# Where attention stops and retention starts: three steps further apart, deferred work kept for its own phase, and retention's first loads in another order

## The chip, the cores and the metric

The kernel runs on one core of one Trainium2 chip, as one launch. The metric is the device time in microseconds (us), as the median of several executions. A core has a matrix engine (PE, with its weight loads shown as PEld), three engines for element work (DVE, ACT, POOL), and a sequencer (SP) that here does nothing but issue DMAs; ACT issues a few DMAs of its own. Each engine takes its instructions in order.

## The reference

One layer that mixes two branches over a sequence of 2048 rows of 1024 columns, all in float32:

```python
h = rms_norm(x, norm_gain[l])
proj = jnp.einsum('bsd,df->bsf', h, w_in[l])
q_a, k_a, v_a, g_a, q_r, k_r, v_r, g_r, m_a, m_r = split_columns(proj)
o_a = chunk_band_attention(q_a, k_a, v_a, rel_bias[l])      # own chunk of 64 rows and 8 to the left, 8 heads
branch_a = (o_a * silu(g_a)) @ w_out_attn[l]
o_r = retention_chunkwise(rotary(q_r), rotary(k_r), v_r, gn_gain[l])   # 8 heads, state carried along the rows
branch_r = (o_r * silu(g_r)) @ w_out_ret[l]
mixed = sigmoid(m_a) * branch_a + sigmoid(m_r) * branch_r
x = x + mixed @ w_out[l]
out = rms_norm(x, final_gain)
```

(Reshapes are left out.) In `retention_chunkwise` the scores of a chunk are multiplied by a decay mask, and a state of 64 by 128 per head goes from chunk to chunk.

## The kernel before, in words

**Two kinds of work share PE.** The large projections are "dense" work: `p0` and `p1` make queries, keys and values of the first and of the second half of the rows, `g0` and `g1` the gates, and `ba`, `br` and `out` the three output products. Each float32 operand is kept as a high and a low part, so one *dense step* is three matmuls of 128x512. A `Strassen` job has chunks of seven products, a product has four steps, and `g0` and `g1` have 14 chunks, thus 392 steps each. Between the dense steps stands the work of attention (`attention`, once for each half of the rows) and of retention (`retention`, likewise). Attention's and retention's Python code emits its own instructions and calls `fill(n)`, which emits n dense steps (fractions are carried in `credit`, of which at most 1.0 is kept). So the order on PE is written out by the program: attention of the first half beside `g0`, then retention of the first half beside the rest of `g0`, and the same for the second half with `g1` and the start of `ba0`.

**What a step leaves for later.** Work that follows a matmul on another engine is put off by whole dense steps: `later(n, fn)` puts `fn` into the list `deferred`, and `step()` runs what is due before it emits the next dense step. A gate's chunk works this way (`ep_gate`: ACT's tanh, DVE's product, and a DMA of the result eight steps later), and so does everything in attention and retention. `flush()` empties the whole list at once. It is called where a phase ends, since the buffers of the phase (`E` tiles, `tr` banks) are given back there: at the end of `p0`, of attention, of retention, of `p1`.

**Refilling the resident operand.** The right-hand operand `R` (seven blocks of 128x4x512, high `r..0` and low `r..1`) stays in the core. While the last chunk of `g0` runs, `reload(n)` refills each block for `p1` as soon as its last product is done: a DMA into the low part (tile `r`), seven or more steps later ACT's copy to the high part, and two steps after that the subtraction on DVE or (every third) on POOL. `fill_yr` does the same at the end of `g1`.

**Attention's end.** `attention` works on units of 256 rows of one head. The last product of a unit (`po`) is emitted `PV_LAG` = 3 steps after its operands, and then ACT, DVE and POOL make the output `oa`, which a DMA writes 6 steps later. `attention` ends with `fill(PV_LAG + 2)`.

**Retention.** `retention` goes over pairs of heads p and stretches st of 256 rows; each of the two heads is an item, 32 in all. For an item PE makes the scores `sr` from `kr` and `qr`; DVE multiplies by the mask `dm` (`sm`), ACT copies the high part (`sh`) and POOL makes the low part (`sl`), one, three and five steps later; two items on, PE makes the output `o` from `sh`, `sl`, `vr` and, where there is a state, from its parts `sstk`. `update` makes the new state (`kv`). Between these stand `fill(RET_FILL)` calls, two for each item, with RET_FILL = 2.1 in the first half and 2.3 in the second. `o` has one PSUM bank, which ACT must have read (`oz` and `o2`) before the next stretch's first output. At the end a short chain of 13 operations on DVE (`rt`) makes the norms. Retention's loads are DMAs on SP: `load_scored` (masks at the first stretch, `kr` in two parts, `qr` in four), `load_valued` (`kd` and two `vr`, and at st = 4 the saved `state` and `sstk`). Before its first scores, `retention` calls `load_scored`, `load_valued`, `load_scored` of the next stretch, and `fill(10)`.

**Names in the profile.** Nearly all instructions are recorded by one helper and bear its line, L139, so they are told apart by their tiles: `ps_g_x` and the like are the dense banks of gates, `ps_p_x` those of projections, `wh` and `wl` the weights' parts, `raw` a chunk's weights as loaded (by ACT's queue), `u` and `c` the sums of a gate's chunk.

Of the kernel before, what the change touches and what calls it, by code (L numbers as in the profile page):

```python
# [55 lines left out]
PR_BUFS = 4  # L56
ATT_FILLS = (1.0, 1.0)
PV_LAG = 3
RET_FILLS = (2.1, 2.3)
ROT_LATE = 10  # L60
PUT = 6
RAW_LEADS = (9, 8)
# [7 lines left out]
def hybrid_kernel(  # L70
# [165 lines left out]
    limit = [1 << 30]  # L236
    hooks = {}

    def later(n, fn):

        order[0] += 1
        deferred.append((steps[0] + n, order[0], fn))
        deferred.sort(key=lambda e: e[:2])

    def put(lag, dst, src):

# [4 lines left out]
        later(n, fn) if ahead[0] else fn()  # L251

    def flush():
        while deferred:
            deferred.pop(0)[2]()

    class Chunk:

# [30 lines left out]
        def matmuls(self, o, ws, rs, start, stop):  # L289
            for k in range(4):  # L290
                mm = lambda a, b, first, last: pe.matmul(
                    o, a[:, k, :], b[:, k, :], start=first, stop=last, skip_group_check=True
                )
                mm(ws[0], rs[0], start and k == 0, False)
                mm(ws[0], rs[1], False, False)
                mm(ws[1], rs[0], False, stop and k == 3)
                if k < 3:
                    yield

        def bank(self, name):  # L300
            if name not in self.ps:
# [128 lines left out]
    def dense(jobs):  # L430
        chunks = [ch for job in jobs for ch in job.chunks]
        following = dict(zip(chunks, chunks[1:]))
        starts = [k for k, (job, ch, n) in enumerate(seq) if isinstance(ch, Plain) and ch.at(n)[2] == 0]
        count, begins = {}, {}
        for at, (job, ch, n) in enumerate(seq):
            if isinstance(ch, Strassen):
                begins.setdefault(ch, at)
        sooner = {at - lead: (ch, [j]) for ch, at in begins.items() for j, lead in enumerate(RAW_LEADS)}
        for at, (job, ch, n) in enumerate(seq):
            count[ch] = count.get(ch, 0) + 1  # L440
            if at in sooner:
                ch2, js = sooner[at]
                if ch2.raw is None or js[0]:
                    len(ch2.raw or ()) == js[0] and ch2.load(js)
            if count[ch] == job.when + 1 and ch in following and following[ch].raw is None:
                following[ch].load()
            prime(at + ahead[0] + 1)
            while starts and starts[0] <= at + job.lead:
                _, ch2, n2 = seq[starts.pop(0)]
                ch2.before(n2)  # L450
            yield from ch.product(n)
            for fn in hooks.get((job.name, ch.c, n), ()):
                fn()
            yield

    def step():
        steps[0] += 1
        while deferred and deferred[0][0] <= steps[0]:
            deferred.pop(0)[2]()
        try:  # L460
            next(stream[0])
        except StopIteration:
            while deferred:
                deferred.pop(0)[2]()
            return False
        return True

    def fill(n):
        credit[0] += n
# [681 lines left out]
    def attention(s, sbp, ps_wide):  # L1151
# [156 lines left out]
        for m in range(len(units) + 1):  # L1308
# [23 lines left out]
            if m:  # L1332
                for _ in weighted(*units[m - 1], prs.pop(m - 1)):
                    fill(ATT_FILL)
        fill(PV_LAG + 2)


    def retention(s, ps_ret):
# [7 lines left out]

        def load_scored(p, st):

            if st == 4 * s:
                load_masks(p)  # L1350
            b, un = st // 2, st % 2
            nm = f"{p}_{st}"
            cc = p // 2
            ks = E(f"kr_{nm}", F32R, (P, 2, T))
            qs = []
            for n in range(2):
                dma(
                    r32(ks[64 * n:64 * n + 64]),
                    r32(krscr[cc][b][un, n, 2 * (p % 2):2 * (p % 2) + 2]).rearrange("i c h t -> (c h) i t"),
                )  # L1360
            for i in range(2):
                q = E(f"qr_{nm}_{i}", F32R, (P, 2, T))
                for half in range(2):
                    dma(
                        r32(q[64 * half:64 * half + 64]),
                        r32(qrscr[cc][b][un, 2 * (p % 2) + i]).rearrange("c h n t -> (c h) n t"),
                    )
                qs.append(q)
            tiles[p, st] = ks, qs

        def load_valued(p, st):
# [6 lines left out]
            for i in range(2):  # L1378
# [3 lines left out]
                )  # L1382
                vs.append(v)
            values[p, st] = vs, kd.rearrange("p i (t c) -> p i t c", t=2)
            if st == 4:
                dma(state.rearrange("p i c -> p (i c)"), stscr[p])
                sstk = epool[0].tile([P, 2, DV], F32R, tag="sstk", bufs=2, name=f"sstk_{p}_{st}")
                dma(r32(sstk).rearrange("p i c -> p (i c)"), r32(skscr[p]))
                sstks[p, 4] = sstk

        def load_masks(p):
            dms[p] = [E(f"dm_{p}_{i}") for i in range(2)]
            for i in range(2):
                dma(dms[p][i], dmask[2 * p + i])

        def scores(p, st, i):

# [67 lines left out]
        def sure(here):  # L1465

            while not here():
                deferred.pop(0)[2]()

        def output(p, st, i, parts, ops):  # L1470
            qs, vs = tiles[p, st][1], values[p, st][0]
# [57 lines left out]
        load_scored(*todo[0])  # L1529
        load_valued(*todo[0])  # L1530
        load_scored(*todo[1])
        pend = None
        items = [(p, st, i) for p, st in todo for i in range(2)]
        fill(10)
        parts = {items[0]: scores(*items[0])}
        fill(RET_FILL)
        parts[items[1]] = scores(*items[1])
# [1 line left out]
        for n, (p, st, i) in enumerate(items):  # L1539
            m = n // 2  # L1540
            if i == 0:
# [2 lines left out]
                    update(p, st)  # L1544
                if m + 1 < len(todo):
                    load_valued(*todo[m + 1])
            fill(RET_FILL)
            if i == 1 and pend:
                pend()
# [199 lines left out]
```

## Time and profile before

| | |
|---|---|
| median of 3 executions | 2006.88 us (2003.42 to 2009.26) |
| the profiled execution, its own time | 2012.78 us |
| its span, from the first to the last instruction | 2011.0 us |
| mean granted TensorE clock | 0.989 |
| PE busy | 1934.4 us, 96% |
| DVE, ACT, POOL busy | 68%, 45%, 44% |
| first retention's first scores / last sums | 605.83 us / 770.38 us |
| second retention's first scores / last output | 1394.86 us / 1563.38 us |

The window view gives busy times, the granted PE clock (PEclk, 1.00 is full speed), and the busy share of the core's 16 DMA engines for stretches of the span. The timeline lists instructions in order of time: start, duration, engine, operation, output and inputs, how many were merged, and in brackets the engine's idle time ahead of it with what ended that. A row of "SPq" or "ACTq" is the issue of a DMA, whose landing comes some us later.

### The profile page before, as it was taken

The numbers are of one execution on the slowest core, as the hardware profiler recorded it, in microseconds if no ns is written. First come the engines' busy times: TensorE is split into PE (matmuls) and PEld (weight loads), VectorE is DVE, ScalarE is ACT, GpSimd is POOL, SyncE is SP. The second block draws the span as 40 slices with busy tenths as digits, with TensorE's granted clock in tenths as the row PEclk, the third lists the DMA queues.
The fourth block names the chain that finished last, engine by engine and source line by source line (L and its number), as shares of the span: only waits on it lengthen the run. The fifth ranks groups of instructions, "written<-read, shape, count | busy, mean of one in ns | idle before, by whom it ended". The sixth has DMA issues, their size and how long they took to land.

```text
span 2011.0 us, 30315 instructions
## 1 busy us (share of the span) xinstructions
PE 1934.4 (96%) x9712; PEld 1609.8 (80%) x9712; DVE 1365.0 (68%) x2603; ACT 900.0 (45%) x1827; POOL 876.7 (44%) x713
## 2 busy tenths in 40 slices
PE   6899999999999999999999999998999999999998
PEld 4687878888878887778788888887888887888886
DVE  7888778677755668888977777765557653644554
ACT  6444554556554556343333555654455311322221
POOL 2543544554556666555644444454565144021000
PEclk9999999999999999999999999999999999999999
DMA  4476796755549987777775645554898999976664
GB/s 147 142 252 201 215 297 210 204 157 165 173 120 278 287 250 261 225 255 237 250 252 179 187 137 179 154 147 149 259 273 261 325 380 364 354 236 211 194 197 136
DMA packets 340910, 447.44 MB, mean 222 GB/s; under 512 B 30776, under 2 KB 194256, under 8 KB 340752
## 3 DMA queue, kind: packets, MB, share of 16 engines
q1 hardware_dynamic: 282688, 388.87, 60.6%
q10 hardware_dynamic: 58064, 56.63, 9.4%
q8 instruction: 78, 1.28, 0.3%
q14 instruction: 80, 0.66, 0.1%
HBM read 294.50 MB, written 150.89 MB: 221 GB/s over the span
## 4 chain that ended last, share of the span: by engine, by line
PE 77%; DVE 9%; DMA 6%; issue 3%; ACT 2%; POOL 1%; SPq 1%; DVEq 0%; ACTq 0%; POOLq 0%
PE ps_g_z L139 7%; PE ps_g_x L139 6%; PE ps_p_z L139 5%; PE ps_p_x L139 5%; PE po L139 4%; PE wide L139 4%; PE ps_g_v L139 3%; PE ps_g_y L139 3%; PE ps_g_w L139 3%; PE o L139 3%; PE ps_p_w L139 3%; PE tp L139 2%; PE ps_p_y L139 2%; PE ps_p_v L139 2%; PE sr L139 1%
## 5 line engine op out<-in xcount | busy, mean ns | idle before, releaser
L139 POOL TENSOR_SCALAR pr<-pr,rsum 128x640 f32<-128x640 f32 (+4 forms) x128 | 96.5, 754 | 235.4 <-DVE rsum L139 104.5
L139 PE MATMUL ps_p_z<-r,wh_p 128*128 128x512 f32 x448 | 146.2, 407 | 8.2 <-DVE u_p L139 5.5
L139 PE MATMUL ps_g_z<-r,wh_g 128*128 128x512 f32 x448 | 143.4, 401 | 2.0 <-DVE c_g L139 1.3
L139 DVE CUSTOM_DVE_ANT_0 pr<-wide,bt 128x640 f32<-128x640 f32 (+4 forms) x128 | 94.2, 736 | 73.5 <-PE wide L139 64.8
L139 PE MATMUL ps_g_x<-r,wh_g 128*128 128x512 f32 x448 | 142.9, 400 | 0.0
L139 PE MATMUL ps_p_x<-r,wh_p 128*128 128x512 f32 x448 | 141.1, 396 | 0.0
L139 ACT ACTIVATE pr<-pr,mn 128x640 f32<-128x640 f32 (+4 forms) x128 | 98.0, 765 | 80.2 <-DVE mn L139 80.2
L139 POOL TENSOR_TENSOR t_p<-raw_p,t_p 128x512 f32<-128x512 f32 x52 | 77.1, 1483 | 127.2 <-DVE wl_p L139 116.4
L139 DVE TENSOR_TENSOR ptl<-tp,pth 128x384 fp32r<-128x384 f32 x168 | 95.7, 571 | 37.0 <-ACT pth L139 35.5
L139 ACT CAST pth<-tp 128x384 fp32r<-128x384 f32 x168 | 85.3, 514 | 75.6 <-PE tp L139 68.3
L139 POOL TENSOR_TENSOR sl<-sm,sh 128x512 fp32r<-128x512 f32 x64 | 86.9, 1359 | 49.4 <-ACT sh L139 36.0
L1096 POOL TENSOR_TENSOR gr<-gr,ta 128x512 f32<-128x512 f32 x32 | 44.6, 1394 | 144.2 <-DVE gr L1095 94.4
L139 PEld LDWEIGHTS ps_p_z<-r,wh_p 128*128 128x128 f32 x448 | 84.0, 194 | 26.8 <-issue 6.2
L139 DVE TENSOR_TENSOR wl_p<-t_p,wh_p 128x512 fp32r<-128x512 f32 x112 | 102.1, 911 | 4.1 <-ACT wh_p L139 3.9
L139 DVE TENSOR_TENSOR sm<-sr,dm 128x512 f32<-128x512 f32 x64 | 44.1, 689 | 83.9 <-PE sr L139 46.6
L139 PEld LDWEIGHTS tp<-ident,pr 128*128 128x128 f32 x560 | 69.5, 140 | 36.5 <-DVE ptl L139 8.7
L139 PEld LDWEIGHTS ps_p_x<-r,wh_p 128*128 128x128 f32 x448 | 83.7, 190 | 18.1 <-DVE r L139 0.7
L139 PE MATMUL tp<-ident,pr 128*128 128x128 f32 x560 | 90.0, 274 | 7.5 <-DVE g L139 2.9
L139 PE MATMUL wide<-ka,qa 128*128 128x512 f32 (+2 forms) x448 | 94.1, 326 | 0.7 <-DVE mn L139 0.7
L139 POOL TENSOR_TENSOR wl_g<-t_g,wh_g 128x512 fp32r<-128x512 f32 x56 | 76.7, 1369 | 38.8 <-ACT wh_g L139 35.0
L139 PE MATMUL po<-pth,va 128*128 128x256 f32 x336 | 92.7, 297 | 0.0
L139 PE MATMUL ps_p_z<-r,wl_p 128*128 128x512 f32 x224 | 89.6, 400 | 1.1 <-DVE wl_p L139 1.1
(1183 smaller groups left out, 5889.0 us busy)
## 6 DMA issues: line engine op xcount, KB each, us to landing
raw_g<-in_w_in_dram ACTq DMA_DIRECT2D x56, 512.0 KB, 5.5
raw_p<-in_w_in_dram ACTq DMA_DIRECT2D x52, 512.0 KB, 6.1
qa<-qas SPq DMA_DIRECT2D x128, 128.0 KB, 2.9
qr<-qrs SPq DMA_DIRECT2D x128, 128.0 KB, 4.5
vr<-vrs SPq DMA_DIRECT2D x64, 256.0 KB, 5.0
ka<-kas SPq DMA_DIRECT2D x40, 256.0 KB, 3.3
va<-vas SPq DMA_DIRECT2D x40, 256.0 KB, 3.2
kds<-kdt_k SPq DMA_DIRECT2D x32, 256.0 KB, 4.3
```

Source lines behind the costliest of these rows:

```text
L139: return tc.keep_in_program_order(op(*a, **k))
L1096: pool.tensor_tensor(g, g, ta, ALU.add)
```

## The change

1. `RET_FILLS` goes from (2.1, 2.3) to (1.9, 2.2): fewer dense steps between the pieces of retention, so its own matmuls stand closer together.
2. `attention` ends with `fill(PV_LAG + 9)` where it had `fill(PV_LAG + 2)`; `retention` has `fill(13)` where it had `fill(10)` before the first scores.
3. Each entry of `deferred` carries a mark, `free`: it is set while a step of a job whose name begins with "g" is emitted, and entries that such an entry makes inherit it. `flush()` emits only the entries without the mark; the others stay in the list until they are due. Gates' results and the refills that hang on a gate's product thus are no longer emitted at once where a phase ends.
4. The masks of the first stretch are loaded after the queries of their head, not ahead of the keys. The load of the saved `state` and `sstk` is a function of its own, `load_state`, which at the start of retention is called after the second stretch's `load_scored`; elsewhere it still follows `load_valued`.

```diff
-RET_FILLS = (2.1, 2.3)
+RET_FILLS = (1.9, 2.2)
...
+    free = [False]
     def later(n, fn):
         order[0] += 1
-        deferred.append((steps[0] + n, order[0], fn))
+        deferred.append((steps[0] + n, order[0], fn, free[0]))
         deferred.sort(key=lambda e: e[:2])
+    def emit(at=0):
+        _, _, fn, was = deferred.pop(at)
+        free[0], was = was, free[0]
+        fn()
+        free[0] = was
...
     def flush():
-        while deferred:
-            deferred.pop(0)[2]()
+        while at := [n for n, e in enumerate(deferred) if not e[3]]:
+            emit(at[0])
...
         for at, (job, ch, n) in enumerate(seq):
+            free[0] = job.name[0] == "g"
...
-            yield from ch.product(n)
+            for _ in ch.product(n):
+                yield True
+                free[0] = job.name[0] == "g"
...
-        fill(PV_LAG + 2)
+        fill(PV_LAG + 9)
...
         def load_scored(p, st):
-            if st == 4 * s:
-                load_masks(p)
...
                 qs.append(q)
+                if st == 4 * s:
+                    load_mask(p, i)
...
         load_scored(*todo[0])
         load_valued(*todo[0])
         load_scored(*todo[1])
+        load_state(*todo[0])
...
-        fill(10)
+        fill(13)
...
                 if m + 1 < len(todo):
                     load_valued(*todo[m + 1])
+                    load_state(*todo[m + 1])
```

`step()` empties the whole list only when the dense stream has ended, as before, and `sure()` takes entries in order, marked or not.

**On PE** the change moves only counts of dense steps, which rows of the order would not show well. Between attention's last `po` and retention's first scores stood 14 dense steps in both halves, and 24 stand there now. Between the first and second scores one fewer stands there now. Within the first retention six places lose two steps each (three times 5 becomes 3, three times 3 becomes 1) and the rest is unchanged; within the second, places gain or lose one step, 6 fewer in all. Before the next projections after the first retention, 118 steps stand where 115 stood.

On SP at the start of the second retention (attention's last output store, `oas`, then the loads; `kr_0_4` is pair 0, stretch 4, and `qr_0_4_1` its second head's queries), before:

```order
L139 DMA oas_3_3_277<-oa_7_3_15760 64x512
L139 DMA dm_0_0_15794<-in_dmask_dram 128x512
L139 DMA dm_0_1_15795<-in_dmask_dram 128x512
L139 DMA kr_0_4_15798<-krs_0_2_184 64x2x256 x2
L139 DMA qr_0_4_0_15801<-qrs_0_2_192 64x512 x2
L139 DMA qr_0_4_1_15804<-qrs_0_2_192 64x512 x2
...
L139 DMA state_15793<-sts_0_459 64x256
L139 DMA sstk_0_4_15814<-sks_0_465 128x256
L139 DMA kr_0_5_15816<-krs_0_2_184 64x2x256 x2
L139 DMA qr_0_5_0_15819<-qrs_0_2_192 64x512 x2
L139 DMA qr_0_5_1_15822<-qrs_0_2_192 64x512 x2
```

The same place on SP in the changed kernel:

```order
L139 DMA oas_3_3_277<-oa_7_3_15760 64x512
L139 DMA kr_0_4_15830<-krs_0_2_184 64x2x256 x2
L139 DMA qr_0_4_0_15833<-qrs_0_2_192 64x512 x2
L139 DMA dm_0_0_15836<-in_dmask_dram 128x512
L139 DMA qr_0_4_1_15838<-qrs_0_2_192 64x512 x2
L139 DMA dm_0_1_15841<-in_dmask_dram 128x512
...
L139 DMA kr_0_5_15849<-krs_0_2_184 64x2x256 x2
L139 DMA qr_0_5_0_15852<-qrs_0_2_192 64x512 x2
L139 DMA qr_0_5_1_15855<-qrs_0_2_192 64x512 x2
L139 DMA state_15829<-sts_0_459 64x256
L139 DMA sstk_0_4_15859<-sks_0_465 128x256
```

The first keys and queries stand two loads earlier, and the second stretch's `kr` and `qr` two loads earlier; the state stands behind them. In the first retention the masks move in the same way.

On ACT at the end of the first retention (`r..0` are copies of refills, `wh_p1_0_4` is a weight of the second product of `p1`, `g_776` and `u3` are gates of the last chunk of `g0`), before:

```order
L139 CAST wh_p1_0_0_9154<-raw_p1_0_0_8958 128x512
L139 CAST r30_87<-r31_88 128x512 x3
L139 CAST r40_89<-r41_90 128x512 x4
L139 CAST r50_91<-r51_92 128x512 x4
L139 ACTIVATE g_776_0_3_0_9205<-ps_g0_13_x_9030 128x512
L139 DMA raw_p1_1_0_9211<-in_w_in_dram 128x4x256
L139 CAST wh_p1_0_4_9213<-t1_p1_0_9087 128x512
```

The same place on ACT in the changed kernel:

```order
L139 CAST wh_p1_0_0_9164<-raw_p1_0_0_8975 128x512
L139 CAST r30_87<-r31_88 128x512 x2
L139 ACTIVATE g_776_0_3_0_9184<-ps_g0_13_x_9030 128x512
L139 CAST r30_87<-r31_88 128x512
L139 DMA raw_p1_1_0_9192<-in_w_in_dram 128x4x256
L139 CAST wh_p1_0_4_9194<-t1_p1_0_9090 128x512
L139 CAST r40_89<-r41_90 128x512 x3
```

Eleven copies stood ahead of `wh_p1_0_4`, and three stand there now. On DVE at the same place, from the first weight of `p1` to its second, before:

```order
L139 TENSOR_TENSOR wl_p1_0_0_9155<-raw_p1_0_0_8958,wh_p1_0_0_9154 128x512
L139 TENSOR_TENSOR r31_88<-r31_88,r30_87 128x512 x2
L139 TENSOR_TENSOR r41_90<-r41_90,r40_89 128x512 x2
L139 TENSOR_TENSOR r51_92<-r51_92,r50_91 128x512 x3
L139 TENSOR_TENSOR u3_g0_13_9142<-ps_g0_13_w_9216,u3_g0_13_9142 128x512
L139 TENSOR_TENSOR wl_p1_0_4_9214<-t1_p1_0_9087,wh_p1_0_4_9213 128x512
```

And in the changed kernel:

```order
L139 TENSOR_TENSOR wl_p1_0_0_9165<-raw_p1_0_0_8975,wh_p1_0_0_9164 128x512
L139 TENSOR_TENSOR r31_88<-r31_88,r30_87 128x512 x2
L139 TENSOR_TENSOR u3_g0_13_9145<-ps_g0_13_w_9197,u3_g0_13_9145 128x512
L139 TENSOR_TENSOR wl_p1_0_4_9195<-t1_p1_0_9090,wh_p1_0_4_9194 128x512
L139 TENSOR_TENSOR r41_90<-r41_90,r40_89 128x512 x2
L139 TENSOR_TENSOR u2_g0_13_9053<-ps_g0_13_z_9064,u2_g0_13_9053 128x512
```

Five of seven refill subtractions moved behind the weight.

More of the change, by code (lines that the diff above doesn't have):

```diff
@@ L297, in matmuls @@
                 if k < 3:
-                    yield
+                    yield True
         def bank(self, name):
@@ L450, in dense @@
                 ch2.before(n2)
-            yield from ch.product(n)
+            for _ in ch.product(n):
+                yield True
+                free[0] = job.name[0] == "g"
             for fn in hooks.get((job.name, ch.c, n), ()):
                 fn()
-            yield
+            yield True
     def step():
@@ L458, in step @@
         while deferred and deferred[0][0] <= steps[0]:
[L459 to L466, printed above, removed]
+            emit()
+        going = next(stream[0], None) is not None
+        free[0] = False
+        while deferred and not going:
+            emit()
+        return going
     def fill(n):
@@ L1384, in load_valued, with load_state @@
             values[p, st] = vs, kd.rearrange("p i (t c) -> p i t c", t=2)
+        def load_state(p, st):
             if st == 4:
@@ L1389, in load_valued, with load_mask @@
                 sstks[p, 4] = sstk
[L1391 to L1394, printed above, removed]
+        def load_mask(p, i):
+            dms.setdefault(p, []).append(E(f"dm_{p}_{i}"))
+            dma(dms[p][i], dmask[2 * p + i])
         def scores(p, st, i):
@@ L1467, in sure @@
             while not here():
-                deferred.pop(0)[2]()
+                emit()
         def output(p, st, i, parts, ops):
```

## The prediction

> **What bounds the kernel now.** The page first: where the chain that ended last goes.
>
> ```profile
> PE 1934.4 (96%) x9712; PEld 1609.8 (80%) x9712; DVE 1365.0 (68%) x2603; ACT 900.0 (45%) x1827; POOL 876.7 (44%) x713
> PE 77%; DVE 9%; DMA 6%; issue 3%; ACT 2%; POOL 1%; SPq 1%; DVEq 0%; ACTq 0%; POOLq 0%
> ```
>
> PE is the bound: 1934.4 of 2011.0 us. The change takes no matmul away, so it can win only where PE idles (76.6 us in all) or runs below full clock. The windows around the places it touches (time; PE, PEld, DVE, ACT, POOL busy; granted clock; DMA share; GB/s):
>
> ```profile
> 600.00:605.00 5.00, 2.34 (x11) 1.60 (x9) 1.29 (x2) 1.24 (x3) 1.26 (x1) 1.00 0.95 248
> 605.00:610.00 5.00, 4.17 (x15) 3.60 (x16) 0.70 (x2) 0.62 (x1) 2.54 (x2) 0.66 1.09 331
> ...
> 790.00:800.00 10.00, 7.70 (x26) 5.56 (x25) 9.84 (x11) 7.49 (x15) 10.00 (x6) 0.83 1.01 327
> ...
> 1405.00:1410.00 5.00, 2.77 (x11) 2.40 (x12) 1.71 (x3) 0.06 (x1) 1.12 (x1) 0.85 1.07 347
> 1410.00:1415.00 5.00, 5.00 (x25) 4.23 (x25) 0.56 (x1) 2.54 (x6) 3.80 (x3) 0.81 0.84 252
> ```
>
> Each place has idle PE and, just behind, a lowered clock. The loss by the clock: 5 x 0.34 = 1.7 us at 605; 10 x 0.17 = 1.7 at 790; 5 x 0.15 + 5 x 0.19 = 1.7 at 1405. The timeline of PE names what ended the idle time at both starts of retention:
>
> ```profile
> 605.83 0.74 PE L139 MATMUL sr<-qr,kr 128*128 128x256 f32 x4 [3.49 <-DMA qr<-qrs]
> ...
> 1387.72 0.62 PE L139 MATMUL ps_g_z<-r,wh_g 128*128 128x512 f32 x2
> 1388.40 0.62 PE L139 MATMUL ps_g_z<-r,wh_g 128*128 128x512 f32 x2
> ...
> 1394.86 0.71 PE L139 MATMUL sr<-qr,kr 128*128 128x256 f32 x4 [1.54 <-DMA qr<-qrs]
> 1402.73 0.40 PE L139 MATMUL o<-qr,sstk 128*128 128x256 f32 x2
> 1407.23 0.71 PE L139 MATMUL sr<-qr,kr 128*128 128x256 f32 x4 [3.38 <-DMA qr<-qrs]
> ```
>
> Retention's first scores wait for queries in both halves, and in the second half the third scores (the second stretch's first) wait again. Successive dense steps begin 1388.40 - 1387.72 = 0.68 us apart: the price of a step.
>
> **The first start of retention.** SP's queue:
>
> ```profile
> 587.67 9.37 SPq L139 DMA_DIRECT2D oas<-oa  x2
> 599.57 2.52 SPq L139 DMA_DIRECT2D qr<-qrs  x4
> ```
>
> SP stands at attention's last store until 597.04 and only then reaches the loads; the first head's two query loads are issued by 599.57 + 1.26 = 600.83, and PE waits from 602.34 to 605.83. The store waits for POOL's `oa`, whose place in the order is unchanged, so the loads start when they did; without the masks ahead of them the first queries leave some 1.0 us sooner. PE arrives ten dense steps later, at 602.34 + 10 x 0.68 = 609.1, which is 3.3 us after the time the data came even with the masks ahead. I count the 3.49 and the 1.7 of clock as gone: -5.2.
>
> **The second start.** SP, ACT's queue, and SP's waits in 1385 to 1415:
>
> ```profile
> 1387.84 0.47 SPq L139 DMA_DIRECT2D oas<-oa  x1
> ...
> 1395.01 0.80 SPq L139 DMA_DIRECT2D state<-sts  x1
> 1399.09 0.32 SPq L139 DMA_DIRECT2D sstk<-sks  x1
> 1399.50 1.26 SPq L139 DMA_DIRECT2D kr<-krs  x2
> 1400.87 2.46 SPq L139 DMA_DIRECT2D qr<-qrs  x4
> ```
> ```profile
> 1392.74 0.41 ACTq L139 DMA_DIRECT2D raw_g<-in_w_in_dram  x1
> ```
> ```profile
> SPq L139 <- DMA raw_g<-in_w_in_dram: 3.3, 1, 3.3
> ```
>
> PE reached the first scores at 1394.86 - 1.54 = 1393.32; it will at 1400.1, 5.3 us after the queries were there. SP then stands 3.3 us, until 1399.09, for a weight load of ACT's queue, with `sstk`, `kr` and `qr` of the second stretch behind it. That load hangs on dense work that does not move, so the wait stays; but `sstk` no longer stands ahead, and `kr` can go at about 1399.1, 0.4 us sooner. From the first scores to the third's place there were 1407.23 - 3.38 - 1394.86 = 9.0 us of work on PE, which stays (one step fewer, one more). PE thus arrives at 1409.1, where the data, 0.4 us sooner than before, come at 1406.8. The 1.54, the 3.38 and the 1.7 go: -6.6.
>
> What is late next is `sstk`, now behind the second stretch's six loads. The first output comes 1402.73 - 1394.86 = 7.9 us after the first scores, at 1408.0. `sstk` is issued at 1399.1 + 1.26 + 0.1 + 2.46 + 0.1 + 0.8 = 1403.8, or a microsecond later if it meets the next weight load; the `qr` that ended the third scores' wait landed 1407.23 - 1400.87 - 1.2 = 5.2 us after its issue, so `sstk` comes between 1407 and 1410. DVE's state update waits for `state` just ahead of it, and behind that on DVE stand the next `sm` and a gate's sum. I take +0.5, ends 0 and +2.
>
> **The end of the first retention.** The flush there emitted the refills at once. PE, ACT, DVE, POOL in turn:
>
> ```profile
> 784.24 0.70 PE L139 MATMUL ps_g_z<-r,wh_g 128*128 128x512 f32 x2 [1.28 <-DVE c_g L139]
> 785.34 0.50 PE L139 MATMUL ps_g_z<-r,wl_g 128*128 128x512 f32 x1 [0.39 <-DVE wl_g L139]
> 792.05 0.74 PE L139 MATMUL ps_p_z<-r,wh_p 128*128 128x512 f32 x2 [1.44 <-ACT wh_p L139]
> 793.65 0.50 PE L139 MATMUL ps_p_z<-r,wl_p 128*128 128x512 f32 x1 [0.87 <-DVE wl_p L139]
> ...
> 806.69 0.50 PE L139 MATMUL ps_p_w<-r,wh_p 128*128 128x512 f32 x1 [0.48 <-POOL r L139]
> ...
> 814.96 0.50 PE L139 MATMUL ps_p_z<-r,wh_p 128*128 128x512 f32 x1 [0.18 <-DVE r L139]
> ```
> ```profile
> 785.70 5.30 ACT L139 CAST r<-r 128x512 fp32r<-128x512 f32 x10
> ```
> ```profile
> 779.58 0.67 DVE L139 TENSOR_TENSOR r<-r,r 128x512 fp32r<-128x512 f32 x1
> 787.62 4.29 DVE L139 TENSOR_TENSOR r<-r,r 128x512 fp32r<-128x512 f32 x7
> ```
> ```profile
> 785.87 12.27 POOL L139 TENSOR_TENSOR r<-r,r 128x512 fp32r<-128x512 f32 x4 [8.68 <-ACT r L139]
> ```
>
> Ten copies on ACT and seven subtractions on DVE stood ahead of the second weight of `p1`, and PE waited 1.44 + 0.87 for it, then ran 1.7 us of clock away. Eight copies (8 x 0.53 = 4.2 us) and five subtractions (5 x 0.61 = 3.1 us) now stand behind: those 4.0 us go. The 1.28 + 0.39 ahead come from DVE's backlog in the `rt` chain, which now begins three dense steps (2.0 us) earlier against the gates, with two more of its operations (1.2 us) ahead: 0.8 goes. That makes -4.8. But the refills are moved, not removed: DVE was busy 9.84 of 10 us in 790 to 800, POOL all of it, and six waits for `r` from 806 to 815 (first and last shown) follow, 2.5 us in all. PE will come there some 3 us sooner and the refills, due to DVE and POOL, will not. I give 1.3 back: -3.5, with ends 0 (everything saved returns as waits for `r`) and -8.2 (all seen there goes: 1.28 + 0.39 + 1.44 + 0.87 + 1.7 + 2.5).
>
> DVE's subtraction takes 0.67 alone, and in 770 to 815:
>
> ```profile
> L139 DVE TENSOR_TENSOR r<-r,r 128x512 fp32r<-128x512 f32 x19 | 17.7, 964 | 0.0
> ```
>
> The mean is 964 ns, and POOL's four took 3.07 each, so the two slow one another. The Trainium skill (SBUF — State Buffer, "SBUF: two separate sides") says that DVE, with two inputs in SBUF, and GpSimd (POOL here) take one shared port pair in turn, as an exclusive lock for the whole instruction. The rows agree that they block each other; by the rule, spreading the refills would free no time on either engine, and the sum with this term at 0 would be -10.0.
>
> On the clock, the rows show three losses of 1.7 us behind idle times of 3.49, 3.38, and 1.44 + 0.87 with 0.74 of work between. The Trainium skill (TensorE: Matmul & The Clock Gate, "What's actually happening") says that half rate follows at least one idle window of about 3.4 us. By the letter only the 3.49 would be charged, and the whole sum would be 3.4 us smaller; the rows show half rate behind shorter ones too, and I go by the rows.
>
> **The retention loops.** Fewer steps mean less cover for the other engines and for loads.
>
> ```profile
> 650.00:750.00 100.00, 98.85 (x584) 86.02 (x584) 64.92 (x112) 53.90 (x107) 66.02 (x51) 1.00 0.91 276
> 1450.00:1550.00 100.00, 100.00 (x589) 87.81 (x588) 62.29 (x106) 55.58 (x104) 62.67 (x48) 1.00 0.94 280
> ```
> ```profile
> 740.98 1.76 POOL L139 TENSOR_TENSOR sl<-sm,sh 128x512 fp32r<-128x512 f32 x1
> ```
> ```profile
> 738.09 0.50 PE L139 MATMUL o<-qr,sstk 128*128 128x256 f32 x2 [0.72 <-ACT o L139]
> 742.82 0.40 PE L139 MATMUL o<-qr,sstk 128*128 128x256 f32 x2
> ```
>
> PE hardly waits in either loop, but the cover is thin: POOL ends `sl` at 742.74 and the output begins at 742.82; one output waited 0.72 for ACT to read `o`. In the first half six places lose two steps, 1.36 us each. If each became a wait in full it would cost 8.2, and it costs 0 where the slack is over 1.4. I take +1.0; in the second half, where places lose one step at most, +0.3 (ends 0 and 2). Moved to other places, the steps cost what they cost now.
>
> **The sum.** -5.2 - 6.6 + 0.5 - 3.5 + 1.0 + 0.3 = -13.5 on the profiled execution's 2012.78, thus 1999.3. That execution is 5.9 above the median of 2006.88; the same difference from the median gives 1993.4.
>
> **Rivals.**
> 1. *The refills give nothing*: DVE and POOL, blocking each other, bound the stretch to 815, and what PE saves at 792 it waits for `r` behind it. For: both full there. Against: what PE waited for at 792 was a weight, not a refill. The third term becomes 0: 1996.9. Chance 0.18.
> 2. *The loops pay most of it back*: the six places wait in full, 8.2 where I have 1.0. For: slack of 0.08 at one output. Against: most places keep their steps. 1993.4 + 7.2 = 2000.6, just at the bound of "same". Chance 0.10.
> 3. *Slower: retention becomes bound by its loads.* The DMA engines are already busy 0.91 and 0.94 in the loops; if they can't be busier, loads take the time they take now, and PE waits for all of the 13 + 6 steps removed, 12.9 us, and behind some four waits of over 2 us it loses 1.7 each, 6.8: 19.7 in place of 1.3, 2011.8. It decides from a loss of 14.8 in the loops on. Against: the windows above at the starts show a share of 1.09, and 13 steps, 8.8 us, out of some 150 us raise 0.91 to about 0.97. Chance 0.06.
> 4. *No change*: SP's waits move with PE and the same idle time returns ten steps later. Against: what SP waited for (POOL's `oa`, a weight load) hangs on dense work that does not move. 2006.9. Chance 0.06.
>
> **Numbers.** The forecast keeps 0.60. Its own range comes from the ends of its terms: best -5.2 - 6.6 - 8.2 = -20.0 (1986.9), worst -5.2 - 6.6 + 2 + 0 + 3 = -6.8 (2000.1). Adding the first two rivals and the spread of three executions (3 us each way) gives 1986 to 2003; outside are the rivals 3 and 4. A measurement of this kernel can tell 0.3%, 6.0 us. Faster by more than that: the forecast, the first rival and a little of the second, 0.81; the same: the rest of the second, and the fourth, 0.12; slower: 0.07.
>
> **What would show it.** Right: first scores of both retentions without a wait for `qr`, no lowered clock behind them; no `wh_p` wait at the end of the first retention, waits for `r` remaining; DMA share in the loops at 0.95 or more with PE over 98% busy. Wrong: PE waits for `sstk`, `sl` or `kr` of over 2 us, a clock loss inside a loop, or DVE and POOL leaving PE as much idle from 780 to 815 as now.

## The result, and the profile after

| | before | changed |
|---|---|---|
| median | 2006.39 us (4 runs, 2003.42 to 2009.26) | 1994.05 us (4 runs, 1991.62 to 1998.08) |
| profiled execution / its span | 2012.78 / 2011.0 us | 1991.62 / 1989.8 us |
| mean granted clock | 0.989 | 0.994 |

The ratio is 0.9936, 95% interval 0.9922 to 0.9949: faster by 12.3 us between the medians. The two profiled executions differ by 21.2 us, so 9 us of what their traces show is the difference of two single executions and not of the kernels. The page of the changed kernel, its busy times and the chain that ended last:

```profile
PE 1926.7 (97%) x9712; PEld 1604.4 (81%) x9712; DVE 1365.6 (69%) x2603; ACT 899.6 (45%) x1827; POOL 878.7 (44%) x713
PE 75%; DVE 9%; DMA 8%; issue 3%; ACT 2%; POOL 2%; SPq 0%; DVEq 0%; ACTq 0%; POOLq 0%
```

PE is still the bound, and 1989.8 - 1926.7 = 63.1 us are idle where 76.6 were. The windows of the changed kernel at the places that the prediction showed (time; PE, PEld, DVE, ACT, POOL busy; granted clock; DMA share; GB/s):

```profile
600.00:605.00 5.00, 5.00 (x26) 4.21 (x25) 1.14 (x3) 2.25 (x4) 4.55 (x4) 1.00 1.05 341
605.00:610.00 5.00, 5.00 (x27) 4.28 (x26) 3.45 (x6) 2.47 (x6) 3.33 (x4) 1.00 1.06 337
...
780.00:790.00 10.00, 8.96 (x38) 6.50 (x37) 10.00 (x11) 8.77 (x17) 7.29 (x5) 1.00 1.05 389
790.00:800.00 10.00, 7.29 (x27) 4.07 (x25) 9.96 (x10) 3.81 (x8) 8.09 (x6) 1.00 0.31 117
...
1400.00:1405.00 5.00, 5.00 (x29) 4.35 (x29) 3.19 (x5) 2.59 (x5) 2.70 (x3) 1.00 0.92 265
...
650.00:750.00 100.00, 100.00 (x605) 88.08 (x604) 67.46 (x118) 56.76 (x110) 68.28 (x52) 1.00 0.89 272
1450.00:1550.00 100.00, 99.80 (x588) 87.34 (x587) 65.22 (x103) 54.82 (x102) 63.74 (x45) 1.00 0.94 284
```

At both starts of retention PE is full at a clock of 1.00; both loops are full too. What is left stands from 770 to 810. The timeline of PE in the changed kernel, first the starts (scores of both halves, and the second half's first output with `sstk`), then the end of the first retention:

```profile
604.25 0.64 PE L139 MATMUL sr<-qr,kr 128*128 128x256 f32 x4
...
1390.33 0.64 PE L139 MATMUL sr<-qr,kr 128*128 128x256 f32 x4
...
1397.93 0.40 PE L139 MATMUL o<-qr,sstk 128*128 128x256 f32 x2
```
```profile
775.18 0.70 PE L139 MATMUL ps_g_z<-r,wh_g 128*128 128x512 f32 x2 [1.48 <-DVE c_g L139]
785.51 0.50 PE L139 MATMUL ps_p_y<-r,wl_p 128*128 128x512 f32 x1 [0.96 <-DVE wl_p L139]
792.42 0.50 PE L139 MATMUL ps_p_x<-r,wl_p 128*128 128x512 f32 x1 [0.99 <-DVE wl_p L139]
...
795.82 0.50 PE L139 MATMUL ps_p_x<-r,wh_p 128*128 128x512 f32 x1 [0.73 <-DVE r L139]
...
804.17 0.50 PE L139 MATMUL ps_p_z<-r,wh_p 128*128 128x512 f32 x1 [0.69 <-POOL r L139]
```

The starts have no bracket: nothing was waited for. At the end of the first retention the wait for `wh_p` is gone, and in its place PE waits for `wl_p` and, seven times, for `r` (the first and the last of 0.96 to 0.99 and of 0.69 to 0.73 are shown); DVE, which makes the `wl_p` and most of the `r`, is busy 10.00 and 9.96 of 10 us.

The sums of PE's waits (of 0.15 us or more) and the lost clock, by place, in the two traces:

| place | before | changed | difference with the clock | forecast |
|---|---|---|---|---|
| first start | 3.49 + 1.7 | 0 | -5.2 | -5.2 |
| rest of the first loop | 1.07 | 0.85 | -0.2 | +1.0 |
| end of the first retention, 765 to 818 | 6.50 + 1.7 | 6.79 | -1.4 | -3.5 |
| second start, `qr` and `sstk` | 4.92 + 1.7 | 0 | -6.6 | -6.6 and +0.5 |
| second loop | 0 (1.07 behind it, at 1557) | 0.20 | +0.2 | +0.3 |

That is -13.2 for the places of the forecast. The rest of the profiled executions' 21.2 lies in `p0`, whose code is the same (23.7 to 20.6, and a loss of clock at 200 us), and in the output products (3.3 to 1.5, and one at 1675).

### The profile page after: what moved, and what is told of

It reads as the page before. It is cut to its first block, busy times and chain, and to the rows that moved or that the text cites. A ratio compares the mean times of both kernels' runs of the same rounds, so it can differ in the third digit from the quotient of the medians.

```text
span 1989.8 us, 30314 instructions
## 1 busy us (share of the span) xinstructions
PE 1926.7 (97%) x9712; PEld 1604.4 (81%) x9712; DVE 1365.6 (69%) x2603; ACT 899.6 (45%) x1827; POOL 878.7 (44%) x713
## 3 DMA queue, kind: packets, MB, share of 16 engines
q8 instruction: 78, 1.28, 0.3%
## 4 chain that ended last, share of the span: by engine, by line
PE 75%; DVE 9%; DMA 8%; issue 3%; ACT 2%; POOL 2%; SPq 0%; DVEq 0%; ACTq 0%; POOLq 0%
PE ps_g_z L139 7%; PE ps_g_x L139 6%; PE ps_p_z L139 5%; PE ps_p_x L139 5%; PE po L139 4%; PE ps_g_w L139 4%; PE wide L139 4%; PE ps_g_v L139 3%; PE ps_g_y L139 3%; PE o L139 3%; PE tp L139 2%; PE ps_p_w L139 2%; PE ps_p_y L139 2%; PE ps_p_v L139 2%; PE sr L139 1%
## 5 line engine op out<-in xcount | busy, mean ns | idle before, releaser
L139 PE MATMUL ps_p_x<-r,wl_p 128*128 128x512 f32 x224 | 87.9, 393 | 1.0 <-DVE wl_p L139 1.0
```

What stands on the lines that cost most here:

```text
L139: return tc.keep_in_program_order(op(*a, **k))
```

## The experiments

The theory was the prediction's sum: cover in dense steps removes the waits at the two starts, the marks remove the wait for the weight at the end of the first retention, and the thinner loops cost a little. The first four kernels each make one part of the change alone.

**Steps alone.** Only the two `fill` calls change.

```diff
-        fill(PV_LAG + 2)
+        fill(PV_LAG + 9)
...
-        fill(10)
+        fill(13)
```

> Of the four parts only the fills: attention ends 7 dense steps later, retention's first scores 3 later; loads, marks and RET_FILLS as before. Theory (the idle time at retention's starts is time in which PE is there before the queries): both starts lose their waits and the two clock losses, since ten steps are 6.8 us and the longest waits were 3.49 and 1.54 + 3.38 us; -11.8 us against the kernel before, ratio 0.994, and the third scores of the second retention do not wait, though their loads still stand behind sstk. Rival (the order of the loads is what removes the second wait): the 3.38 us wait for qr and its 1.7 us of clock stay, -6.7 us, ratio 0.9967. The end of the first retention stays as before in both (6.5 us of waits and 1.7 us of clock).

Measured: 1996.42 us, 0.9959 (0.9944 to 0.9974), somewhat less gain than the 0.994 expected. The starts came out as the theory had it, the second without any wait though the loads kept their old order. Not foreseen was the end of the first retention (PE's timeline, then ACT's copies of refills):

```profile
605.39 0.71 PE L139 MATMUL sr<-qr,kr 128*128 128x256 f32 x4 [0.40 <-issue]
...
780.30 0.50 PE L139 MATMUL ps_p_z<-r,wl_p 128*128 128x512 f32 x1 [1.90 <-DVE wl_p L139]
789.34 0.80 PE L139 MATMUL ps_p_y<-r,wl_p 128*128 128x512 f32 x1 [6.01 <-DVE wl_p L139]
798.08 1.22 PE L139 MATMUL ps_p_v<-r,wh_p 128*128 128x512 f32 x2 [4.56 <-ACT wh_p L139]
```
```profile
780.13 6.86 ACT L139 CAST r<-r 128x512 fp32r<-128x512 f32 x13
```

The ten steps move retention's end against the refills: the flush now emits thirteen copies in a row, and this place costs 12.5 us of waits where it cost 6.5, and 6.8 us of clock where it cost 1.7 (the granted clock was 0.50 from 786.5 to 792.5 and from 796.5 to 803). So the waits there are no fixed price that an edit removes; they depend on where the phase's end falls. By the two traces the starts (-11.4), this place (+11.1) and the attention of the second half (-2.1) leave only 2.4 us of gain, by the times it is over 8; traces of single executions do not settle that difference.

**Marks alone.** The marks and this; everything else is as before.

```diff
     def flush():
-        while deferred:
-            deferred.pop(0)[2]()
+        while at := [n for n, e in enumerate(deferred) if not e[3]]:
+            emit(at[0])
```

> Of the four parts only the marks: a flush leaves gates' work in the list; fills, loads and RET_FILLS as before. Theory: the starts of retention keep their waits for qr (3.49 and 1.54 + 3.38 us, two clock losses of 1.7 us); at the end of the first retention the wait for the weight wh_p goes, waits for r grow, the clock loss of 1.7 us there goes; -2 to -3 us, ratio 0.9985 to 0.999. Rival (a flush that emits gates' work early is what delays the loads at the starts): the starts get better too, -8 us or more, ratio 0.996. Second rival (DVE and POOL bound the end of the first retention): 0, ratio 1.000.

Measured: 2002.13 us, 0.9992 (0.9978 to 1.0005): no difference that can be told. The wait for `wh_p` is gone, as expected, but 6.2 us of waits remain from 765 to 818 (1.28 for `c_g`, 0.40 for `wl_g`, 0.34 and 0.99 for `wl_p`, and seven for `r`, 3.2 in all), and 1.7 us of clock is lost there as before (0.95 and 0.71 in the windows from 775 to 785). Not foreseen was the second start: the first two scores wait 1.55 and 0.66 us, but the third scores do not wait, and no clock is lost.

```profile
1397.27 0.64 PE L139 MATMUL sr<-qr,kr 128*128 128x256 f32 x4
```

Order of loads and number of steps are those of the kernel before, where these scores waited 3.38. So that wait is no fixed price of the old order.

**Loads alone.** Only the order of retention's first loads changes.

```diff
-            if st == 4 * s:
-                load_masks(p)
...
                 qs.append(q)
+                if st == 4 * s:
+                    load_mask(p, i)
...
         load_scored(*todo[1])
+        load_state(*todo[0])
```

> Of the four parts only the order of the loads: masks behind the queries, state and sstk behind the second stretch's loads; fills, marks and RET_FILLS as before. Theory: the first queries leave about 1.0 us sooner, so the first waits shrink from 3.49 to about 2.5 and from 1.54 to about 0.5 us; the third scores' wait shrinks by 0.4 us, from 3.38 to about 3; the clock losses stay where over 2 us of waiting stays; -2.4 us, ratio 0.9988. Rival (the order of the loads is most of the gain): waits gone at the second start, -6 us or more, ratio 0.997.

Measured: 2009.34 us, 1.0022 (1.0011 to 1.0033): slower, where the theory had -2.4 us. PE's timeline (the first start's first scores, the second start's second scores, and the first output with the saved state), and the window behind the last wait:

```profile
602.88 0.92 PE L139 MATMUL sr<-qr,kr 128*128 128x256 f32 x4 [1.94 <-DMA qr<-qrs]
...
1393.98 0.71 PE L139 MATMUL sr<-qr,kr 128*128 128x256 f32 x4 [0.65 <-DMA qr<-qrs]
...
1404.79 0.47 PE L139 MATMUL o<-qr,sstk 128*128 128x256 f32 x2 [4.52 <-DMA sstk<-sks]
```
```profile
1405.00:1410.00 5.00, 5.00 (x22) 4.41 (x22) 3.03 (x7) 0.98 (x3) 0.00 (x0) 0.66 0.98 302
```

The queries do come sooner: the first scores wait 1.94 in place of 3.49, those of the second half no longer wait (1.54 before), the second scores there wait 0.65, and the 3.38 is gone. But the saved state comes 4.52 us late, and 5 x 0.34 = 1.7 us of clock follows. The forecast's bound for that wait was 2 us, with the steps in place.

**Thinner loops alone.**

```diff
-RET_FILLS = (2.1, 2.3)
+RET_FILLS = (1.9, 2.2)
```

> Of the four parts only RET_FILLS at 1.9 and 2.2; 13 and 6.6 dense steps leave the retention loops and stand in the projections that follow. Theory: a cost of 1.3 us in the loops, bounds 0 and 8: ratio 1.0006, between 1.000 and 1.004; the starts keep their waits. Rival (denser loops are a gain of their own, since DVE's closing chain of retention meets fewer refills): -2 us or more, ratio 0.999 or less.

Measured: 2007.17 us, 1.0013 (1.0001 to 1.0024): slower by some 2 us, at the bound of what can be told. The loops hold no wait over 0.28; the first start waited 3.96, the second 1.28 and 1.31 for `qr` at its first and second scores, and nothing at its third: here too the 3.38 is gone, though neither the loads nor the steps ahead of them were edited.

The next four kernels are the changed kernel with one part undone.

**Full flush again.**

```diff
-        while at := [n for n, e in enumerate(deferred) if not e[3]]:
-            emit(at[0])
+        while deferred:
+            emit()
```

> The changed kernel with a flush that empties the whole list again. Theory (the marks spread the refills behind the first retention; with the fills alone, waits of 1.90, 6.01 and 4.56 us and two clock losses of 3.4 us stood there): the starts stay free of waits, and the end of the first retention costs 2 to 8 us more than the 6.8 us of the changed kernel; against the kernel before -4 to -10 us, ratio 0.995 to 0.998. Rival (DVE and POOL bound that stretch whatever the order): as the changed kernel, ratio 0.9936.

Measured: 1996.73 us, 0.9954 (0.9939 to 0.9970). Its PE at the end of the first retention:

```profile
783.65 0.97 PE L139 MATMUL ps_p_x<-r,wh_p 128*128 128x512 f32 x2 [3.71 <-ACT wh_p L139]
787.71 0.79 PE L139 MATMUL ps_p_x<-r,wl_p 128*128 128x512 f32 x1 [3.10 <-DVE wl_p L139]
```

There the marks save 9.3 - 6.8 = 2.5 us of waits, and 3.4 of clock (the window 780 to 790 was granted 0.70 here and 790 to 795 0.92, both 1.00 in the changed kernel). That is as the theory had it. The times agree in sign, 2.7 us, but the intervals overlap. The first start is not quite free: its second scores wait 0.70 us for `qr`.

**Old order of loads.**

```diff
+            if st == 4 * s:
+                for i in range(2):
+                    load_mask(p, i)
...
-                if st == 4 * s:
-                    load_mask(p, i)
...
-        load_scored(*todo[1])
         load_state(*todo[0])
+        load_scored(*todo[1])
```

> The changed kernel with the loads in their old order (masks first, state and sstk ahead of the second stretch). Theory (ten dense steps cover either order; the load order alone moved the wait from qr to sstk): as the changed kernel, ratio 0.9936, no wait over 0.5 us at either start. Rival (the new order is needed for the third scores of the second retention): a wait for qr of about 1 to 3 us there, perhaps with 1.7 us of clock, ratio 0.995.

Measured: 1995.23 us, 0.9949 (0.9933 to 0.9966). No wait at either start, as the theory had it; the rest of the first loop has 2.4 us of waits where the changed kernel's trace has 0.85. With the steps in, the order of loads is worth nothing that can be told.

**Old RET_FILLS**, measured twice, the second time beside the changed kernel once more.

```diff
-RET_FILLS = (1.9, 2.2)
+RET_FILLS = (2.1, 2.3)
```

> The changed kernel with RET_FILLS at 2.1 and 2.3 again. The first retention then ends some 13 dense steps later against the gates, up to the limit of the dense work. Theory (what RET_FILLS is worth lies at the end of the first retention: its closing chain on DVE meets the refills, and with the fills alone 12.5 us of waits stood there): 3 to 9 us more than the changed kernel, ratio 0.995 to 0.998. Rival (fewer steps in the loops cost 1.3 us): 1.3 us less than the changed kernel, ratio 0.993.

> The changed kernel with RET_FILLS back at (2.1, 2.3), measured once more beside the changed kernel on one chip, to settle what the thinner retention loops cost. Theory, from the first measurement (0.9918 of the kernel before, the changed kernel 0.9936): the steps taken out of the loops cost about 3 to 4 us, so 0.9915 to 0.9925 here with the changed kernel at 0.9930 to 0.9945. Rival (the forecast's own terms, 1.0 + 0.3): a difference of about 1.3 us, within the intervals of both. The wait for queries inside the second loop, 1.6 us in the first profile, should be there again if it belongs to the order and not to chance.

> The changed kernel as it is, again, as the mark for the other kernels of this chip. 0.9936 of the kernel before by the first measurement; 0.9925 to 0.9950 if that holds. Both starts of retention without a wait for queries or for the saved state; 6 to 7.5 us of waits on PE from 765 to 810 us, DVE full there.

Measured: 1990.01 us, 0.9918 (0.9904 to 0.9932), and again 1990.18, 0.9930 (0.9919 to 0.9942), where the changed kernel had 1995.21, 0.9955 (0.9940 to 0.9971). So the thinner loops cost 4.0 and 5.0 us between the medians (each pair of intervals overlaps a little, and both point the same way), and my first theory, that the old RET_FILLS would cost 3 to 9 us, fell. The changed kernel came out as expected at the starts and at the end of the first retention (6.8 us of waits); its ratio is just above the expected range. The wait for queries in the second loop of the kernel with the old RET_FILLS, 1.63 us in the first trace, is there again with 1.10, so it belongs to the order. Yet neither trace of the changed kernel shows this in a loop. It stands 350 us and more later, in the attention of the second half. PE's `tp` (transposes of the probabilities) from 1100 to 1375 us, for the changed kernel and for the one with the old RET_FILLS; the number behind the bar's second part is PE's idle time ahead of it:

```profile
L139 PE MATMUL tp<-ident,pr 128*128 128x128 f32 x320 | 51.5, 275 | 5.3 <-DVE ptl L139 2.6 <-POOL pr L139 1.4 <-DVE g L139 1.2
```
```profile
L139 PE MATMUL tp<-ident,pr 128*128 128x128 f32 x320 | 51.4, 274 | 2.8 <-POOL pr L139 1.4 <-DVE g L139 0.9 <-DVE ptl L139 0.5
```

The steps that the loops no longer hold are not lost; all dense work behind them stands elsewhere against attention, whose code is untouched, and this I take to be the cause. The fourteen traces of this study fall in two groups: the four with 24 steps at the starts and RET_FILLS (2.1, 2.3) have 3.0 to 3.1 us of waits from 1100 to 1380, the other ten 5.1 to 5.5. That accounts for 2.4 of the 4 to 5 us. For the rest I have no place: the spans of the profiled executions differ by only 0.1 (1989.8 and 1989.7) and 1.9 us (1990.0 and 1988.1).

The two traces with the old RET_FILLS also show what the marks are worth beside the steps. The kernel with the steps alone differs from this one in the marks and in the order of loads, which by the run above is worth nothing here. At the end of the first retention it had 12.5 us of waits and 6.8 of clock; this kernel has 7.2 and 1.7 in the first trace, and 6.0 and 3.4 in the second, whose ACT makes three copies where thirteen stood (ACT, then PE):

```profile
781.73 1.65 ACT L139 CAST r<-r 128x512 fp32r<-128x512 f32 x3
```
```profile
781.90 0.50 PE L139 MATMUL ps_p_z<-r,wl_p 128*128 128x512 f32 x1 [1.91 <-DVE wl_p L139]
788.40 0.50 PE L139 MATMUL ps_p_y<-r,wl_p 128*128 128x512 f32 x1 [1.89 <-DVE wl_p L139]
```

That is some 10 us in the traces. The times say 0.9918 and 0.9930 against 0.9959, 6 to 8 us, and neither interval meets that of the steps alone (0.9944 to 0.9974).

**Old steps.**

```diff
-        fill(PV_LAG + 9)
+        fill(PV_LAG + 2)
...
-        fill(13)
+        fill(10)
```

> The changed kernel with 14 dense steps again between attention and retention. Theory: the wait for qr returns at the first start (about 2 us, as with the new load order alone) and a wait for sstk of about 4.5 us at the second, each with 1.7 us of clock; 8 to 10 us more than the changed kernel, ratio 0.998 to 0.999. Rival (the marks let the loads go sooner): waits under 1 us at the starts, 0 to 3 us more, ratio 0.994 to 0.995.

Measured: 2008.29 us, 1.0012 (1.0002 to 1.0022), above the expected 0.998 to 0.999. Without the steps nothing of the gain is left. The waits are about those of the theory; in both halves the first scores no longer wait, and it is the second scores that do. PE's timeline:

```profile
602.67 0.81 PE L139 MATMUL sr<-qr,kr 128*128 128x256 f32 x4 [2.33 <-DMA qr<-qrs]
...
1390.95 0.71 PE L139 MATMUL sr<-qr,kr 128*128 128x256 f32 x4 [1.27 <-DMA qr<-qrs]
...
1402.31 0.77 PE L139 MATMUL o<-qr,sstk 128*128 128x256 f32 x2 [3.85 <-DMA sstk<-sks]
```

**Half the steps.** 19 where before had 14 and the changed kernel 24.

```diff
-RET_FILLS = (1.9, 2.2)
+RET_FILLS = (2.1, 2.3)
...
-        fill(PV_LAG + 9)
+        fill(PV_LAG + 5)
...
-        fill(13)
+        fill(12)
```

> RET_FILLS (2.1, 2.3), attention's last fill PV_LAG + 5 where the changed kernel has PV_LAG + 9, and retention's first fill 12 where it has 13: 19 dense steps between attention's last product and the first scores, where before had 14 and the changed kernel 24. Theory (the loads come at a time of their own, and each step covers 0.68 us of them): with 14 steps the changed kernel waited 2.33 at the first start and 1.27 + 0.70 + 0.30 + 3.85 = 6.1 at the second; five steps cover 3.4. So no wait at the first start, and 2 to 3 us for sstk at the second, with perhaps 1.7 of clock behind it: about 1992.5 to 1995. Rival (the loads' order on SP moves with PE, so that cover only counts when it is whole): waits of 2 us or more at both starts, 1996 to 2002. Second rival (19 are enough everywhere): no wait of over 1 us, 1990.

Measured: 1998.68 us, 0.9966 (0.9954 to 0.9979). No wait for `qr` at either start; the second start waits for the state alone, less than expected:

```profile
1401.25 0.48 PE L139 MATMUL o<-qr,sstk 128*128 128x256 f32 x2 [1.70 <-DMA sstk<-sks]
```

The loads thus come at a time of their own, and cover counts in parts, as the theory had it: by their waits both rivals fall. The time is 4 us above the expected range, inside the first rival's; beside the kernel with 24 steps and the same RET_FILLS, the trace has more waits at the end of the first retention (8.3 us against 7.2 and 6.0 in its two traces), four for `vr` in the first loop (1.9 in all), and more in the attention of the second half (5.1 against 3.0). The expectation counted the starts alone.

**All refills on DVE**, with RET_FILLS (2.1, 2.3).

```diff
-            later(1, lambda k=k, t=t: refill(m, k, cscr[m][k], 7 + 4 * t // 3 - 4 * at, pool if t % 3 == 2 else dve))
+            later(1, lambda k=k, t=t: refill(m, k, cscr[m][k], 7 + 4 * t // 3 - 4 * at, dve))
```

> RET_FILLS (2.1, 2.3), and all refill subtractions on DVE, where every third was POOL's. In the profile of the changed kernel with the old RET_FILLS, DVE did 18 of them from 765 to 815 us in 18.1 us (1024 ns each, 0.67 us where nothing else is beside them), and POOL 9 in 15.8 us. Theory (the two engines hold each other up, so POOL's share saves DVE nothing): 27 on DVE at 0.67 take 18.1 us, the same as 18 now; waits on PE from 765 to 810 stay at 5 to 8 us (7.4 before), the time within 2 us of that kernel's (1990). Rival (POOL's work is a real help and the longer subtractions come from something else): DVE gets 9 x 0.67 = 6.0 us more work in a stretch where it is full, PE's waits grow to 12 us or more and 1.7 us of clock is lost once or twice more: 1996 to 1999.

Measured: 1986.88 us, 0.9913 (0.9900 to 0.9927), the fastest of all; the changed kernel had 0.9955 (0.9940 to 0.9971) on the same chip. The groups from 770 to 815 us, first with all refills on DVE, then with every third on POOL (the old RET_FILLS in both):

```profile
L139 DVE TENSOR_TENSOR r<-r,r 128x512 fp32r<-128x512 f32 x25 | 18.4, 765 | 0.0
```
```profile
L139 DVE TENSOR_TENSOR r<-r,r 128x512 fp32r<-128x512 f32 x17 | 16.4, 981 | 0.2 <-ACT r L139 0.2
...
L139 POOL TENSOR_TENSOR r<-r,r 128x512 fp32r<-128x512 f32 x8 | 14.1, 1756 | 11.1 <-ACT r L139 11.1
```

Eight more subtractions cost DVE 2.0 us and save POOL 14.1; PE's waits from 765 to 818 are 5.0 us against 6.0 (7.2 in the other trace of that kernel). POOL's share of the refills was no help: the rival's 12 us of waits did not come. Whether it also gains is at the edge: 3.3 us between the medians, with intervals that overlap.

## Why the prediction came out as it did

**The starts** were right in mechanism, and in size between the two traces: -5.2 and -6.6. How far the second holds beyond them stays open: 3.38 + 1.7 of it is the wait of the third scores, which the traces of the marks alone and of the thinner loops alone do not have, though their loads and the steps ahead are those of before. These two kernels wait 2.5 and 2.6 us at the second start in all, without a loss of clock, where the kernel before waited 4.9 and lost 1.7. The experiments add which edit does it. The steps alone clear both starts; the order of loads alone, the marks alone or the thinner loops alone leave 1.9 to 4.0 us at the first. The wait of SP for ACT's weight load, which the forecast said would stay, stayed, and cost nothing. SP's queue in the changed kernel at the second start:

```profile
1384.27 1.27 SPq L139 DMA_DIRECT2D vr<-vrs  x2
1388.61 1.26 SPq L139 DMA_DIRECT2D kr<-krs  x2
1389.92 3.01 SPq L139 DMA_DIRECT2D qr<-qrs  x4
1392.97 0.60 SPq L139 DMA_DIRECT2D state<-sts  x1
1393.61 0.58 SPq L139 DMA_DIRECT2D sstk<-sks  x1
```

SP issued nothing from 1385.5 to 1388.6, 3.1 us.

**`sstk`** cost 0, in the forecast's bounds of 0 and +2 (I took +0.5). It was issued 1397.93 - 1393.61 = 4.3 us ahead of its use; the forecast had 1408.0 - 1403.8 = 4.2. That may be little: where PE waited for it, the output began 2.4 us (half the steps, issued at 1398.83), 4.0 us (the loads alone, issued at 1400.79) and 5.5 us (the old steps, issued at 1396.77) after the issue. My worst case did not look at the kernel without the steps, where it is 3.85 and 4.52 late: the steps are the gain, and the new order of loads is harmless only where they stand.

**The end of the first retention** is where the sum was wrong. The step that failed is "Eight copies and five subtractions now stand behind: those 4.0 us go", with only 1.3 given back. The wait for `wh_p` (1.44) went and came back in full, as waits for `wl_p` (0.87 before, 1.95 after) and `r` (2.5 and 3.2); the 0.8 that was to go from the waits for `c_g` and `wl_g` ahead did not go either (1.67 and 1.64). In all it is 6.50 before and 6.79 after; the term is -1.4, all of it clock. That is the first rival's mechanism: PE is as much idle over the whole place as before. DVE has little free time there (busy 50.5 and 53.7 of the 55 us from 765 to 820), and PE must get its weight parts and refills from it. I had the row that says so (9.84 of 10 us) and still priced most of the reordering as a gain.

Yet the marks are not worth nothing, and here the forecast missed a gain. Both the steps and the loops move this place: with the clock, steps alone cost 12.5 + 6.8 us, marks alone 6.2 + 1.7, thinner loops alone 5.9 + 1.7, full flush with the rest 9.3 + 3.4. I costed the marks against the alignment of before, which the same change abolishes. There they gain little; with the steps in, they save what the steps would lose here.

That DVE and POOL slow each other was in the forecast's rows, and the run with all refills on DVE bears it out: 765 ns for one where it was 981 beside POOL. The Trainium skill (SBUF — State Buffer, "SBUF: two separate sides") says that the two engines take a shared port pair in turn. By that rule the term would have been 0 and the sum -10.0; measured was -1.4.

**The loops.** +1.0 and +0.3 in the loops were too much (-0.2 and +0.2 in the trace, DMA share 0.89 and 0.94, not the 0.95 or more that I named). But the price of the edit, seen from the kernel that has the steps, was too small: 4 to 5 us, of which 2.4 lie in the attention of the second half. The step that failed is "Moved to other places, the steps cost what they cost now".

**The total.** -12.3 between the medians against -13.5: the forecast holds, but by errors that offset each other: the end of the first retention was taken 2.1 us too good, the loops 1.3 and `sstk` 0.5 too bad (-13.5 + 2.1 - 1.3 - 0.5 = -13.2, the sum of the table). What RET_FILLS costs could not show in this total: the attention of the second half waits 5.1 us before and 5.5 after, and the change only missed the 2.4 that the steps bring there with the old RET_FILLS. So the total is in part luck: the two places that carry it, the starts, came as forecast, and the errors elsewhere happened to cancel.

**On the clock** I went by the rows, which showed losses behind waits of less than 3.4 us. The Trainium skill (TensorE: Matmul & The Clock Gate, "What's actually happening") asks for an idle window of about 3.4 us. These runs differ from that, and the measurement decides: here is the window behind a lone wait of 1.97 us in the kernel with thinner loops alone, its PE first.

```profile
1588.17 0.73 PE L139 MATMUL ps_ba_(0, 0)_18211<-r,wh_ba_(0, 0)_18138 128*128 128x512 f32 x2 [1.97 <-ACT wh_ba_(0, 0)_18138 L285]
```
```profile
1585.00:1590.00 5.00, 3.04 (x13) 1.85 (x12) 2.88 (x6) 1.14 (x2) 0.00 (x0) 0.99 1.05 400
1590.00:1595.00 5.00, 5.00 (x17) 3.96 (x16) 2.84 (x5) 0.00 (x0) 1.39 (x2) 0.67 0.98 341
```

## What to carry to other kernels

Where a phase's first work waits for loads that start when the phase before ends, put independent work between the two, and count it: here five steps of 0.68 us each took the second start's waits from 6.1 to 1.7 us, so cover counts even when there is too little of it. Putting loads in order of use helps the first and delays the last; check the last against its own use before taking it as free. Where one engine makes most of what the bound engine waits for and is nearly full, another order of its work may only rename the wait, as the marks did at the old place of the phase's end (6.5 and 6.2 us); at the place where the steps put that end, the same marks saved some 10 us. So price an edit at the alignment that the whole change makes, and look for the cost of moved work also where the next phases meet it.

## What the runs showed of the hardware

The granted clock falls to a half for a piece of about 3.4 us (at the first start of the kernel before it was 0.50 in every half microsecond from 606.0 to 609.5, and 5 x 0.34 = 1.7 us were lost), and it does so behind idle times much shorter than that. One limit on a single wait does not explain it. It fell behind lone waits of 1.97 us (above), 1.94 (first start with the loads alone: 0.82 and 0.84 in the two windows around it) and 1.89 (old RET_FILLS, first trace, at 780: 0.66 from 780 to 785). It did not fall behind 2.16 at 786 in that same trace (1.00 from 785 to 795), nor behind the 1.90 at 780 with the steps alone (1.00 from 780 to 785), not behind the 1.70 for `sstk` with half the steps (1.00 in the windows from 1400 to 1410), not behind 1.48 and 0.96 in the changed kernel, yet behind 1.58 and, 1.5 us later, 0.39 in the kernel with all refills on DVE:

```profile
859.17 0.66 PE L139 MATMUL trva<-ident,c_p 128*128 128x128 f32 x4 [1.58 <-DVE c_p L139]
861.02 0.48 PE L139 MATMUL trkr_k<-ident,u_p 128*128 128x128 f32 x1 [0.39 <-DVE u_p L139]
```
```profile
860.00:865.00 5.00, 4.61 (x17) 3.46 (x16) 5.00 (x8) 3.23 (x8) 1.67 (x1) 0.66 0.56 152
```

And 1.28 + 0.39 with work between lost no clock at 785 in the kernel before, while 1.28 + 0.40 did at 780 with the marks alone (0.71 in 780 to 785). So waits of 1.9 to 2.2 us were charged in some places and not in others; what decides stays open.
